# Interleaving the high and the low part of each weight chunk element by element in one tile, in a fp32 decoder trunk

## The chip, the cores and the metric

The kernel runs on one core of a Trainium2 chip. The metric is the device time of one execution in microseconds (us), as the median of three runs; lower is better. Engines are named as in the profile: PE is the matmul engine and PEld its weight loads, DVE the vector engine, ACT the scalar engine, POOL the general one, and SP the engine from whose queue the weight transfers are issued.

## The reference

Two layers of a decoder block work on one sequence of 256 tokens with a width of 1024. A layer is a half-weighted SwiGLU feed-forward part (FFN), a mixer, and a second FFN; each is preceded by an RMS norm, and shifted, scaled and gated by vectors that are computed from a condition `c`. What matters of it:

```python
for l in range(DEPTH):
    mod = jnp.split(c_act @ w_ada[l] + b_ada[l], N_MOD, axis=-1)
    h = modulate(rms_norm(x, ffn1_norm[l]), mod[0], mod[1])
    x = x + FFN_RESIDUAL * (1 + mod[2])[:, None, :] * swiglu(h, ffn1_w_gu[l], ffn1_w_down[l])
    h = modulate(rms_norm(x, mix_norm[l]), mod[3], mod[4])
    y = hybrid_mixer(h, cos, sin, w_in[l], q_a_norm[l], w_uq[l], kv_a_norm[l], w_ukv[l],
                     conv_w[l], attn_out_norm[l], conv_out_norm[l], w_o[l])
    x = x + (1 + mod[5])[:, None, :] * y
    h = modulate(rms_norm(x, ffn2_norm[l]), mod[6], mod[7])
    x = x + FFN_RESIDUAL * (1 + mod[8])[:, None, :] * swiglu(h, ffn2_w_gu[l], ffn2_w_down[l])
return rms_norm(x, final_norm)
```

The mixer projects `h` once, sends one part of the columns through latent attention with 8 heads and the other through a gated convolution of three taps, norms both and projects the pair. All data are fp32, and so is the answer. The hidden width of a FFN is 2816.

## The kernel before

Features lie on the 128 partitions and tokens along the free dimension, so a weight tile of 128x128 is the stationary operand of a matmul and the activations of 256 tokens are the moving one.

**Three matmuls for one product.** Both operands are split into a high part, rounded to the type F32R (a reduced fp32 that PE multiplies in one pass), and a low part, the rest: w = hi + lo and a = aH + aL. `mm3` (L282) issues hi\*aH, hi\*aL and lo\*aH into the same accumulator, and leaves lo\*aL out. All of them go through `mm` (L277), whose line of issue, L279, is therefore the line of nearly all matmuls in the profile.

**The weight stream.** The weights come as chunks of 128x2048 fp32, 16 tiles each (1 MB). `load` (L234) takes the next chunk of a fixed list: it allocates a tile `raw` for the transfer and two tiles `hi` and `lo` for its parts, each of three buffers, issues the transfer on SP (L244), issues the condition's rows that are due (`ada`, L188, a multiply and sum on DVE over 128x1024), and splits the chunk in two or four pieces. For each piece ACT copies `raw` to `hi` (L254, in `top`), and DVE subtracts: `lo` = `raw` - `hi` (L257, in `rest`). The chunks of the first FFN come first, then those of the mixer, then those of the second FFN.

**Who reads hi and lo.** The projections, the FFNs and the attention's queries and keys read them as stationary operands. One place reads them as the moving operand: `values` (L629), where PE takes `ckvH` and `ckvL` as stationary tiles and streams 512 columns of `hi` or `lo`, twelve matmuls in each layer. Four tiles of each of the first eight chunks are not split at all, but multiplied from `raw` in full fp32.

**What sets the order.** The kernel gives each piece of work a due time (`due`, L273), counted in nominal matmul time, and a scheduler orders the instructions of ACT, DVE and (in the FFNs) PE by due time and by when their operands would be ready. SP's order is written by hand everywhere, PE's in the mixer, where it follows `ORDER` (L42). At the end of a mixer stands the output projection `out` (L743). Its last step (a `B` of `ORDER`) brings the last two of the eight residual tiles, `residual` (L373, its sum at L376), and `put` (L366) makes the next FFN's input from them: `uH` on ACT (L334) and `uL` on DVE (L340). The first chunk of that FFN starts before all of that input is there, since its matmuls take the feature tiles k = 0 to 7 in turn (L481 to L483).

Of the kernel before, what the change touches and what calls it, by code (L numbers as in the profile page):

```python
# [12 lines left out]
F32R = mybir.dt.float32r  # L13
# [5 lines left out]
P = 128  # L19
# [12 lines left out]
CH = 16 * P  # L32
# [86 lines left out]
def trunk(ctx: ExitStack, tc, x_d, c_d, pos_d, small_d, cst_d, ada_d, gu1_d, dn1_d, win_d, up_d, wo_d, gu2_d, dn2_d, out_d):  # L119
# [9 lines left out]
    def nm(s):  # L129
        uid[0] += 1  # L130
        return f"{s}_{uid[0]}"
# [11 lines left out]

# [1 line left out]
    x = one.tile([P, KD, S], F32, name="x")  # L145
# [23 lines left out]

# [1 line left out]
    mods = [one.tile([P, NA], F32, name=f"mod{l}") for l in range(L)]  # L171
# [19 lines left out]
    def ada_target(i):  # L191
        """Rows of the modulation that are due by chunk i."""
        for (a, u), (b, v) in zip(PACE, PACE[1:]):
            if i <= b:
                return min(u + (v - u) * max(i - a, 0) // (b - a), len(ADA_ORDER))
        return len(ADA_ORDER)
# [6 lines left out]
    def last_of():  # L203
        """The last instruction so far of the vector and the scalar engine."""
        o = nc.cur_bb.bb.instructions
        return [next(i for i in reversed(o) if i.engine == e) for e in (mybir.EngineType.DVE, mybir.EngineType.Activation)]

# [1 line left out]
    stream = []  # L209
# [24 lines left out]
    def load(apart=False):  # L234
        """Loads the next chunk and splits it, at once or by the functions that come with it."""
        i = taken[0]
        taken[0] += 1
        src, n, cuts = stream[i][:3]
        z0 = stream[i][3] if len(stream[i]) > 3 else 0
        raw = wp.tile([P, CH], F32, tag="raw", name=nm("raw"), bufs=3)  # L240
        hi = wp.tile([P, CH], F32R, tag="hi", name=nm("hi"), bufs=3)
        lo = wp.tile([P, CH], F32R, tag="lo", name=nm("lo"), bufs=3)
        due(-LOAD_LEAD)
        nc.sync.dma_start(raw[:, :n], src)  # L244
        due(lead[1])
        with ExitStack() as es:
            for q in guard:
                es.enter_context(tc.issue_after(q))
            ada(ada_target(i + 1))
        c = (n - z0) // cuts  # L250
        zs = [slice(z0 + q * c, z0 + (q + 1) * c) for q in range(cuts)]

        def top(q):
            nc.scalar.activation(hi[:, zs[q]], raw[:, zs[q]], AF.Copy)  # L254

        def rest(q):
            nc.vector.tensor_tensor(lo[:, zs[q]], raw[:, zs[q]], f32(hi[:, zs[q]]), ALU.subtract)  # L257

        if apart:
            return (raw, hi, lo), top, rest  # L260
        with ExitStack() as es:
            for q in guard:
                es.enter_context(tc.issue_after(q))
            for q in range(cuts):
                due(c / 128 * 322 * q - lead[0])
                top(q)
                rest(q)
        return raw, hi, lo
# [4 lines left out]
    def due(t):  # L273
        """What follows is wanted t ns after the matmuls so far."""
        tc.cur_priority = int(clock[0] + t)
# [14 lines left out]

# [1 line left out]
    class Stat:  # L292
        """Sum of squares over the features, then 1/sqrt(mean + eps) on every partition."""

# [15 lines left out]
        def rstd(self, r, ps=None, then=None, t=0):  # L310
            """Leaves 1/sqrt(mean + eps) in r, and the table of the function that is next."""
            more = ps is not None
# [16 lines left out]
    def warm(src, func):  # L329
        """Loads the table of func ahead of its use, once src is there."""  # L330
        nc.scalar.activation(work([P, 1], "warm", 2), src, func)
# [10 lines left out]
    class Pre:  # L342
        """Input of a sub-layer: x*g*(1+scale) in two parts, the shift in two more columns."""

# [26 lines left out]

# [1 line left out]
    def residual(src, m, l, sub, f):  # L373
# [12 lines left out]
    def ffn(l, sub, pre, nxt, first=False):  # L386
        def evac(j, pg, pu, r):
            """Activation of pair j from PSUM, in two parts."""
            sg = work([P, S], "cc", 3)
# [16 lines left out]
        if first:  # L406
            r = work([P, S], "r", 1)
# [124 lines left out]
    def mixer(l, pre, nxt):  # L532
# [12 lines left out]
        def scaled(pt):  # L545
            """Brings two tiles of the projection from PSUM."""
            b = work([P, 2], "pb", 4)
# [20 lines left out]
        def proj(t, evac):  # L568
            """A quarter of two tiles of the projection."""
            n = seen[t] = seen.get(t, -1) + 1  # L570
# [11 lines left out]

        # q and kv latents
        def kv_evac(gb):
# [23 lines left out]

        # keys without position, values
        def keys():  # L610
# [31 lines left out]

        # attention, two heads at a time
        hd = [dict() for _ in range(4)]
# [68 lines left out]

        # gated short convolution
        def conv_evac(gb):
# [23 lines left out]

        # output projection  # L740
        acc = []
# [37 lines left out]

# [1 line left out]
    def rope():  # L781
# [63 lines left out]

# [1 line left out]
    fin = Stat(D)  # L847
# [12 lines left out]
def _tiles(w):  # L860
    """[.., K, M] -> [.., K/128, M/128, 128, 128]"""
    k, m = w.shape[-2:]
    w = w.reshape(w.shape[:-2] + (k // P, P, m // P, P))
    return np.swapaxes(w, -3, -2)
# [72 lines left out]
```

## Time and profile before

| what | us |
|---|---|
| median of 3 runs | 1005.36 (1004.75 to 1005.51) |
| span of the profiled execution, first to last instruction | 1002.8 |
| median less span: what lies around the span | 2.6 |
| PE busy | 976.1 |
| DVE busy | 809.7 |
| ACT busy | 551.5 |
| `lo` on DVE (L257), 384 instructions | 394.8 |
| `hi` on ACT (L254), 384 instructions | 338.4 |

A group's row names the line, the engine, the operation, the tile written and the tiles read, the shapes and the count, and after the bar the busy time in us, the mean of one in ns, and the idle time of the engine just before it. A row of a window names the stretch in us, and for each engine its busy time and its number of instructions in it. A row of the timeline begins with the start in us and the duration. Records of matmuls overlap, as PE is pipelined, so the pace is read from their starts or their number in a window, and not from their durations.

### The profile page before, as it was taken

How to read it: one execution, taken by the hardware profiler on the slowest of the kernel's cores; microseconds unless marked ns; L12 is line 12 of the kernel's file. 1: busy time of each engine (PE TensorE's matmuls, PEld its weight loads, DVE VectorE, ACT ScalarE, POOL GpSimd, SP SyncE). 2: the span in 40 equal slices, each digit the busy share in tenths (PEclk: the TensorE clock that was granted, in tenths of full speed). 3: DMA queues.
4: the chain of work that ended last, by engine and by line, in shares of the span. 5: the costliest groups of instructions: out<-in, count | busy, mean ns of one | idle time of the engine just before them, and what ended most of it. 6: DMA issues, size and time to landing. Idle time of an engine off the chain costs nothing.

```text
span 1002.8 us, 19512 instructions
## 1 busy us (share of the span) xinstructions
PE 976.1 (97%) x7982; PEld 960.6 (96%) x7982; DVE 809.7 (81%) x1518; ACT 551.5 (55%) x958; POOL 8.0 (1%) x27
## 2 busy tenths in 40 slices
PE   6999999999989999999999999999999999999996
PEld 4999999999989999999999999999998999999996
DVE  5999999899999987777889777778898998645452
ACT  5464544468856744454475444445787585444441
POOL 0000020000000000000000000000000000000000
PEclk9999999999999999999999999999999999999999
DMA  8989889873755678777758778776464447554531
GB/s 329 367 343 359 315 320 348 292 297 138 275 182 210 262 297 292 261 289 273 277 226 313 270 261 292 283 270 228 149 226 189 169 174 307 193 198 181 179 116 42
DMA packets 46442, 250.42 MB, mean 250 GB/s; under 512 B 5441, under 2 KB 5761, under 8 KB 25874
## 3 DMA queue, kind: packets, MB, share of 16 engines
q1 hardware_dynamic: 45938, 248.95, 67.4%
q8 instruction: 62, 1.02, 0.4%
q0 software_dynamic: 416, 0.25, 0.1%
q14 instruction: 26, 0.21, 0.1%
HBM read 248.07 MB, written 1.10 MB: 248 GB/s over the span
## 4 chain that ended last, share of the span: by engine, by line
PE 92%; DVE 5%; issue 1%; ACT 1%; DMA 1%; SPq 0%; DVEq 0%
PE ps L279 91%; DVE lo L257 1%; DMA x<-in_x 1%; PE ps L695 1%; DVE x L376 1%; DVE ada L188 0%; DVE acc L305 0%; DVE nt L558 0%; DVE mr L338 0%; DVE uL L340 0%; DVE rs_a L326 0%; ACT hi L254 0%; DVE rs_a L325 0%; ACT rs_y L321 0%; DVE y L383 0%
## 5 line engine op out<-in xcount | busy, mean ns | idle before, releaser
L279 PE MATMUL ps<-uH,hi 128*128 128x256 f32 (+1 forms) x1664 | 472.4, 284 | 0.0
L279 PE MATMUL ps<-uH,lo 128*128 128x256 f32 (+1 forms) x1664 | 469.4, 282 | 0.0
L279 PE MATMUL ps<-uL,hi 128*128 128x256 f32 x1664 | 465.5, 280 | 0.6 <-DVE uL L340 0.6
L257 DVE TENSOR_TENSOR lo<-raw,hi 128x1024 fp32r<-128x1024 f32 (+2 forms) x384 | 394.8, 1046 | 78.2 <-ACT hi L254 77.3
L254 ACT ACTIVATE hi<-raw 128x1024 fp32r<-128x1024 f32 (+2 forms) x384 | 338.4, 913 | 214.2 <-PE ps L279 134.0
L279 PEld LDWEIGHTS ps<-uL,hi 128*128 128x128 f32 x1664 | 315.1, 189 | 1.5 <-DVE uL L340 1.0
L279 PEld LDWEIGHTS ps<-uH,lo 128*128 128x128 f32 x1664 | 313.6, 188 | 0.0
L279 PEld LDWEIGHTS ps<-uH,hi 128*128 128x128 f32 x1664 | 312.5, 188 | 1.1 <-issue 0.3
L188 DVE CUSTOM_DVE_ANT_0 ada<-ada,cb,small 128x1024 f32<-128x1024 f32 x144 | 182.9, 1280 | 47.1 <-DMA ada<-in_ada 47.0
L279 PE MATMUL ps<-aH,hi 128*128 128x256 f32 x704 | 199.5, 283 | 0.0
L279 PE MATMUL ps<-aL,hi 128*128 128x256 f32 x704 | 197.8, 281 | 0.0
L279 PE MATMUL ps<-aH,lo 128*128 128x256 f32 x704 | 197.7, 281 | 0.0
L279 PEld LDWEIGHTS ps<-aL,hi 128*128 128x128 f32 x704 | 132.5, 188 | 0.0
L279 PEld LDWEIGHTS ps<-aH,hi 128*128 128x128 f32 x704 | 132.3, 188 | 0.0
L279 PEld LDWEIGHTS ps<-aH,lo 128*128 128x128 f32 x704 | 132.1, 188 | 0.0
L279 PE MATMUL ps<-mr,hi 128*128 128x256 f32 x384 | 73.2, 291 | 6.2 <-ACT mr L334 3.1
L279 PEld LDWEIGHTS ps<-mr,hi 128*128 128x128 f32 x384 | 61.4, 195 | 8.4 <-ACT mr L334 3.5
L334 ACT ACTIVATE aH<-cc 128x256 fp32r<-128x256 f32 x88 | 36.3, 415 | 55.6 <-DVE cc L392 51.9
L279 PE MATMUL ps<-mr,lo 128*128 128x256 f32 x192 | 55.0, 287 | 0.0
L334 ACT ACTIVATE uH<-x,gs 128x256 fp32r<-128x256 f32 x40 | 20.2, 505 | 57.7 <-DVE x L376 57.7
L376 DVE SCALAR_TENSOR_TENSOR x<-ps,gate,x 128x256 f32<-128x256 f32 x48 | 22.4, 480 | 25.6 <-PE ps L279 25.6
L391 ACT ACTIVATE cc<-ps 128x256 f32<-128x256 f32 x76 | 27.9, 368 | 24.4 <-PE ps L279 23.5
(117 smaller groups left out, 622.0 us busy)
## 6 DMA issues: line engine op xcount, KB each, us to landing
raw<-in_gu SPq DMA_DIRECT2D x88, 1024.0 KB, 5.3
ada<-in_ada SPq DMA_DIRECT2D x144, 512.0 KB, 6.0
raw<-in_dn SPq DMA_DIRECT2D x44, 1024.0 KB, 5.4
raw<-in_win SPq DMA_DIRECT2D x18, 1024.0 KB, 5.1
raw<-in_wo SPq DMA_DIRECT2D x8, 1024.0 KB, 4.9
raw<-in_up SPq DMA_DIRECT2D x2, 1024.0 KB, 5.2
raw<-in_up SPq DMA_DIRECT2D x2, 768.0 KB, 5.2
raw<-in_up SPq DMA_DIRECT2D x4, 384.0 KB, 3.3
```

The lines of the kernel that those rows point to most:

```text
L188: nc.vector.tensor_tensor_reduce(out=a, in0=a, in1=cb, scale=1.0, scalar=sm(l, t), op0=ALU.mult, op1=ALU.add, accum_out=mods[l][:, t:t + 1])
L254: nc.scalar.activation(hi[:, zs[q]], raw[:, zs[q]], AF.Copy)
L257: nc.vector.tensor_tensor(lo[:, zs[q]], raw[:, zs[q]], f32(hi[:, zs[q]]), ALU.subtract)
L279: nc.tensor.matmul(dst, a, b, **kw)
L334: nc.scalar.activation(dH, src, AF.Copy, scale=scale)
L376: nc.vector.scalar_tensor_tensor(x[:, m, :], src, g, x[:, m, :], ALU.mult, ALU.add)
L391: nc.scalar.activation(sg, pg, AF.Silu)
L695: nc.tensor.transpose(ps[:, e, z], d["e"][:, e, z], ident)
```

## The change

`load` allocates one tile `both` of 128x2048x2 F32R values in place of the two tiles. Element 0 of each pair is the high part and element 1 the low part, so `hi` and `lo` are views of the same tile with a step of two elements, 8 bytes.

```diff
         raw = wp.tile([P, CH], F32, tag="raw", name=nm("raw"), bufs=3)
-        hi = wp.tile([P, CH], F32R, tag="hi", name=nm("hi"), bufs=3)
-        lo = wp.tile([P, CH], F32R, tag="lo", name=nm("lo"), bufs=3)
+        both = wp.tile([P, CH, 2], F32R, tag="hl", name=nm("hl"), bufs=3)
+        hi, lo = both[:, :, 0], both[:, :, 1]
```

The rest of the code is the same, apart from comments; the bytes of SBUF are the same too. Every reader and writer of a part now steps over the other part: the copy to `hi` on ACT writes with that step, the subtraction on DVE reads one operand and writes its result with it, and the weight loads of PE read with it, as do the moving operands of `values`.

The number of instructions on each engine and what they do is unchanged, and the order on SP and POOL too. On ACT, DVE and PE the scheduler places some instructions differently. On DVE the first such place is in the first layer's first FFN, behind the last steps of the rope tables. `lo` and `hl` are the low part of a chunk (L257), `cc` and `aL` belong to the activation of a pair of hidden tiles (L392 and L338), `ada` is a row of the condition (L188) and `gs` a column of scales. Before:

```order
L783 SCALAR_TENSOR_TENSOR ro_806<-ro_812 128x32
L188 ISA ada_1451,mod_87<-ada_1451,cb,small 128x1024
L188 ISA mod_87 128x1
L392 TENSOR_TENSOR cc_1312<-ps_1263,cc_1312 128x256
L257 TENSOR_TENSOR lo_1449<-raw_1447,hi_1448 128x1024
L338 TENSOR_TENSOR aL_622<-cc_1312,aH_621 128x256
L257 TENSOR_TENSOR lo_1449<-raw_1447,hi_1448 128x1024
```

With the change, at the same place:

```order
L783 SCALAR_TENSOR_TENSOR ro_795<-ro_801 128x32
L392 TENSOR_TENSOR cc_1295<-ps_1246,cc_1295 128x256
L188 ISA ada_1431,mod_87<-ada_1431,cb,small 128x1024
L188 ISA mod_87 128x1
L338 TENSOR_TENSOR aL_614<-cc_1295,aH_613 128x256
L257 TENSOR_TENSOR hl_1429<-raw_1428,hl_1429 128x1024 x2
```

The activation of the pair now stands ahead of the condition's row and of both halves of the chunk's low part, where it stood between them. The same exchange is seen in the rows that follow, and on ACT.

On PE the order differs where the first layer's mixer hands over to its second FFN. The tile `mr` holds the inputs of the output projection, so `mr` rows are its last step (24 matmuls), and rows with `uH` and `uL` are the FFN's first chunk. Before, the seam where that step begins, with 15 matmuls of the FFN ahead of it:

```order
L279 MATMUL ps_3843<-uH,hi_3833 128x258 [waits Activation_49]
L279 MATMUL ps_3843<-uL,hi_3833 128x256 [waits DVE_49]
L279 MATMUL ps_3843<-uH,lo_3834 128x258
L279 MATMUL ps_3508<-mr_2422,hi_3612 128x256 [waits DVE_49]
L279 MATMUL ps_3508<-mr_2422,hi_3612 128x256
L279 MATMUL ps_3508<-mr_2422,lo_3613 128x256
```

With the change, 24 matmuls of the FFN stand ahead of it:

```order
L279 MATMUL ps_3792<-uL,hl_3783 128x256
L279 MATMUL ps_3792<-uH,hl_3783 128x258
L279 MATMUL ps_3460<-mr_2389,hl_3563 128x256 [waits DVE_49]
L279 MATMUL ps_3460<-mr_2389,hl_3563 128x256 x23
L279 MATMUL ps_3792<-uH,hl_3783 128x258 [waits Activation_49]
L279 MATMUL ps_3792<-uL,hl_3783 128x256 [waits DVE_49]
```

So nine matmuls of the FFN moved ahead of the mixer's last step. In the second layer one matmul moved in the same way.

## Prediction

> **What bounds the kernel now.** I read the page first, for the busy times and the chain that ended last, then the windows, for the stages.
>
> ```profile
> span 1002.8 us, 19512 instructions
> PE 976.1 (97%) x7982; PEld 960.6 (96%) x7982; DVE 809.7 (81%) x1518; ACT 551.5 (55%) x958; POOL 8.0 (1%) x27
> PE 92%; DVE 5%; issue 1%; ACT 1%; DMA 1%; SPq 0%; DVEq 0%
> 20.00:60.00 40.00, 40.00 (x299) 38.73 (x298) 35.77 (x63) 21.17 (x31) 0.00 (x0) 1.00 0.93 352
> 60.00:210.00 150.00, 150.00 (x1258) 149.82 (x1257) 139.27 (x271) 72.82 (x119) 6.69 (x13) 1.00 0.88 333
> 210.00:300.00 90.00, 86.96 (x694) 83.30 (x694) 84.22 (x210) 66.56 (x151) 0.40 (x4) 1.00 0.57 205
> 300.00:500.00 200.00, 198.59 (x1663) 197.92 (x1662) 168.65 (x284) 107.27 (x170) 0.00 (x0) 1.00 0.73 270
> 500.00:700.00 200.00, 200.00 (x1681) 199.89 (x1680) 159.83 (x262) 103.50 (x162) 0.00 (x0) 1.00 0.73 268
> 700.00:900.00 200.00, 196.68 (x1599) 192.57 (x1598) 164.88 (x348) 128.39 (x253) 0.20 (x2) 0.99 0.55 200
> 900.00:1003.00 103.00, 93.78 (x783) 92.98 (x781) 47.26 (x65) 40.91 (x60) 0.00 (x0) 0.98 0.38 133
> ```
>
> The columns of a window are its length, then busy time and count of PE, PEld, DVE, ACT and POOL, the granted clock, and the DMA's share and rate. PE is the bound: it carries 92% of the chain, and from 60 to 900 us it lacks only 3.0 + 1.4 + 3.3 = 7.7 us, in the windows with the two mixers. Its pace in the first of the long windows is 150 us / 1258 = 119.2 ns for a matmul, at full granted clock. Beside it DVE is the next: 139.27 of 150 us there, so 10.7 us to spare, but 31 to 40 us in each of the three windows of 200 us. ACT has half of its time free.
>
> **What the change does, part by part.** No instruction is added or taken away; four kinds of access now step over 8 bytes for each fp32 value, and some instructions stand in another order. So the sum is one of prices of a step. I take each kind in turn: the weight loads, the copies and subtractions, the moving operands, the order.
>
> ```profile
> L279 PEld LDWEIGHTS ps<-uL,hi 128*128 128x128 f32 x1664 | 315.1, 189 | 1.5 <-DVE uL L340 1.0
> L279 PEld LDWEIGHTS ps<-uH,lo 128*128 128x128 f32 x1664 | 313.6, 188 | 0.0
> L279 PEld LDWEIGHTS ps<-uH,hi 128*128 128x128 f32 x1664 | 312.5, 188 | 1.1 <-issue 0.3
> L279 PEld LDWEIGHTS ps<-aL,hi 128*128 128x128 f32 x704 | 132.5, 188 | 0.0
> L279 PEld LDWEIGHTS ps<-aH,hi 128*128 128x128 f32 x704 | 132.3, 188 | 0.0
> L279 PEld LDWEIGHTS ps<-aH,lo 128*128 128x128 f32 x704 | 132.1, 188 | 0.0
> L279 PEld LDWEIGHTS ps<-mr,hi 128*128 128x128 f32 x384 | 61.4, 195 | 8.4 <-ACT mr L334 3.5 <-DVE x L376 2.5 <-DVE mr L338 1.4
> L279 PEld LDWEIGHTS ps<-mr,lo 128*128 128x128 f32 x192 | 37.4, 195 | 0.0
> L279 PEld LDWEIGHTS ps<-mf,qh 128*128 128x128 f32 x64 | 9.2, 191 | 0.9 <-issue 0.3
> L279 PEld LDWEIGHTS ps<-pT,mf 128*64 128x64 f32 x64 | 4.0, 136 | 2.5 <-ACT cc L554 0.7
> 235.68 0.39 PE L279 MATMUL ps<-lo,mr 128*128 128x512 f32 x1
> 236.37 0.39 PE L279 MATMUL ps<-lo,mr 128*128 128x512 f32 x1
> ```
>
> *Weight loads.* The first eight rows are the loads of `hi` and `lo`: 3 x 1664 + 3 x 704 + 384 + 192 = 7680. One load stands to each matmul and runs beside the one before, so a load that comes to stick out by 1 ns costs 7.7 us in all. No row has a stepped load. Lower bound: 0. Upper bound: the stream of a load doubles. The last two load rows give that stream: 64 columns more take 191 - 136 = 55 ns, 0.86 ns a column, 110 ns for 128; so at most 7680 x 110 ns = +845 us. I take 0, by the moving operand as the nearest row. In `values` (the two timeline rows) three matmuls of 512 columns take 236.37 - 235.68 = 0.69 us, so PE draws a contiguous row of fp32 at 0.45 ns a value, or 8.9 bytes of address range per ns. A stepped load at its present pace covers 8 bytes in 0.86 ns, 9.3 per ns, nearly the same. If what costs is how much of a partition's memory a port crosses in a ns, a load is at a rate that another port of the same engine already keeps up.
>
> ```profile
> L257 DVE TENSOR_TENSOR lo<-raw,hi 128x1024 fp32r<-128x1024 f32 x252 | 304.8, 1219 | 74.0 <-ACT hi L254 73.4 <-issue 0.3
> L257 DVE TENSOR_TENSOR lo<-raw,hi 128x512 fp32r<-128x512 f32 x104 | 67.0, 684 | 1.1 <-ACT hi L254 0.9
> L783 DVE TENSOR_TENSOR ro<-ro,ro 128x32 f32<-128x32 f32 x2 | 0.4, 183 | 0.0
> L364 DVE TENSOR_TENSOR uH<-mod,uH 128x8 fp32r<-128x8 f32 x5 | 0.8, 167 | 0.0
> L254 ACT ACTIVATE hi<-raw 128x1024 fp32r<-128x1024 f32 x252 | 260.8, 1053 | 195.0 <-PE ps L279 126.0 <-issue 65.8 <-DMA raw<-in_dn 1.6
> L254 ACT ACTIVATE hi<-raw 128x512 fp32r<-128x512 f32 x104 | 58.0, 619 | 13.0 <-PE ps L279 5.4 <-issue 3.5 <-DMA raw<-in_win 2.8
> L363 ACT ACTIVATE uH<-mod 128x8 fp32r<-128x8 f32 x5 | 1.0, 204 | 1.3 <-DVE mod L188 1.3
> L331 ACT ACTIVATE warm<-cc 128x1 f32<-128x1 f32 x4 | 0.8, 203 | 0.0
> ```
>
> *Subtractions on DVE.* A column costs (1219 - 684) / 512 = 1.045 ns now, so the stepped access covers 8 / 1.045 = 7.7 bytes per ns, less than the moving operand. Lower bound: 0. The nearest stepped row is L364, which reads one operand and writes its result with a step of a whole row (258 values), on 8 values. By L783 a contiguous one of 8 would take 183 - 24 x 1.045 = 158 ns; it takes 167, so 9 / 8 = 1.1 ns a value more. That is the upper bound, with a far longer step and a count so small that the 9 ns may be something else. I take 0; what a price would do is the first rival. The Trainium skill, page "SBUF — State Buffer", section "Specifications (TRN2)", says that memory lines are 16 bytes and two hits in a line are enough for full bandwidth. By that, a step of 8 bytes, which hits each line twice, is free on every engine, the sum stays as it is, and L364, whose step leaves the line, would pay, as its 9 ns allow.
>
> *Copies on ACT.* (1053 - 619) / 512 = 0.85 ns a column, 9.4 bytes per ns when stepped. L363 writes 8 values with the long step in 204 ns, where L331 writes a single one in 203, so its row shows no price: lower bound 0; upper bound a doubling, 0.85 ns x 329,728 columns (252 x 1024 + 104 x 512 and 28 smaller pieces) = 280 us more work on an engine with 451 us free. I take 0.
>
> *Moving operands.* Of all matmuls 24 take 512 stepped values as moving operand, at 0.23 us each. Here the stepped access would cover 17.8 bytes per ns, twice what any row shows. Lower bound 0, upper bound a doubling: 24 x 0.23 = +5.5 us, straight on PE, which runs without a break there. I take 0 as the likeliest and hold the 5.5 us as a case of its own.
>
> *The order.* In the FFNs a chunk's split comes ahead of its use by more than an exchange of two instructions of 0.4 and 1.2 us; from 500 to 700 us PE never stops. At the mixers' end there is no such cover:
>
> ```profile
> 319.09 0.87 DVE L376 SCALAR_TENSOR_TENSOR x<-ps,gate,x 128x256 f32<-128x256 f32 x2
> 319.88 1.22 DVE L257 TENSOR_TENSOR lo<-raw,hi 128x1024 fp32r<-128x1024 f32 x1
> 321.54 0.39 PE L279 MATMUL ps<-uL,hi 128*128 128x256 f32 x1 [0.27 <-DVE uL L340]
> ```
>
> PE already waits 0.27 us for the last `uL`, which comes from the last residual by way of DVE, behind a subtraction. With nine matmuls put ahead of the step that brings the residual, 9 x 0.119 = 1.1 us, that `uL` comes up to 1.1 us later, and nothing else is left for PE to do meanwhile; in the second layer it is 0.1 us. Lower bound: -0.3 us (the wait goes), upper bound +1.2 us. DVE's order is new there too; I take the middle, +0.7 us.
>
> *Sum.* 1002.8 + 0 + 0 + 0 + 0 + 0.7 = 1003.5 us of span, and 2.6 us around it (the median of 1005.36 less the span) give 1006.1, so **1006 us**. About 0.2%, 2 us, is what a measurement of this kernel tells from no change.
>
> **The rivals.**
>
> *DVE becomes the bound (slower).* Place: the first FFN, 60 to 210 us, then every window up to 900. The first window holds some 51,700 columns of subtraction (61.5 us by the first row below, at 1219 / 1024 = 1.19 ns with the fixed part), so the point from which it decides is 10.7 us / 51,700 = 0.21 ns more a column, a fifth more.
>
> ```profile
> 60.00:210.00 150.00, 61.50 (x54) 1.00 0.88 333
> 300.00:500.00 200.00, 84.97 (x72) 1.00 0.73 270
> 500.00:700.00 200.00, 85.13 (x76) 1.00 0.73 268
> 700.00:900.00 200.00, 78.45 (x86) 0.99 0.55 200
> 900.00:1003.00 103.00, 33.68 (x28) 0.98 0.38 133
> L257 DVE TENSOR_TENSOR lo<-raw,hi 128x1024 fp32r<-128x1024 f32 (+2 forms) x384 | 394.8, 1046 | 78.2 <-ACT hi L254 77.3
> ```
>
> The first five rows are L257's share of DVE, the last its whole. At 1.1 ns more, each of these times grows by 1.1 / 1.19 = 92%. DVE then needs 196 us in the first window, and 247, 238 and 237 in the next three; after 900 us it has room. The rest, 394.8 - 343.7 = 51.1 us, lies nearly all between 20 and 60 and between 210 and 300 us; it grows by 47, where DVE has 130 - 120 = 10 us to spare. That is 46 + 47 + 38 + 37 + 37 = +205 us, 1211 in all. At half the price it is 18 + 8 + 0 + 1 + 13 = +40 us, 1046. For it: two of the three operands are stepped, and L364 may show a price. Against: the same row is tiny, and 7.7 bytes per ns is the slowest of the four kinds of access. The Trainium skill, page "Vector Engine (DVE) Microarchitecture Reference", section "5.2 Measured stream behaviour on trn2 (trn3 not measured)", speaks for this rival: a port keeps its full rate only over runs of two adjacent words, and a result that hops at every value took 1.71 ns a column against 1.05. An estimate by these figures, 0.66 ns more, would put this kernel near 1077 us. That page and the other disagree for a step of two words, and no row here settles it. Chance 0.17.
>
> *The weight loads stick out (slower).* If a stepped load takes 13 ns longer than the present pace hides, a ninth of 119 ns, it costs 100 us (1106); a doubled stream 845 us (1851). For it: PE has nothing to hide it behind, and 119.2 ns is only 4 ns above what 256 columns take at 0.45 ns (115), so a load that is nearly as long as its matmul has little slack. Against: the range per ns, above. Chance 0.14.
>
> *Only the moving operands pay (slower).* 1006.1 + 5.5 = 1011.6. For it: twice the highest rate that any row shows. Against: that the highest rate shown is the limit isn't shown. Chance 0.20.
>
> *The new order frees PE (faster).* At most the 7.7 us that PE lacks between 60 and 900 us could go: 998 to 1003. Against: these waits hang on activations and norms, which the change leaves as they are, and at the one seam that I can follow it goes the other way. Chance 0.06.
>
> That the change doesn't do what it says is not a case here: the order shows one tile in the place of two at every reader.
>
> **How the numbers follow.** No price that can be measured has 0.43 and is the likeliest single case; its own range is 1004 to 1008. The slower cases together hold more, 0.17 + 0.14 + 0.20 = 0.51; faster 0.06. So the likeliest case's own range is not the range: that goes from 1003, which cuts off most of the faster case, to 1106, which holds the moving operands, DVE at up to about half its price and somewhat more, and the loads at 13 ns. Left out are about 0.05 of DVE's chance, 0.08 of the loads', and 0.04 below.
>
> **What would show it.** Right: L257 and L254 of 128x1024 stay at 1219 and 1053 ns, the pace in a FFN window stays at 119 ns, the matmuls of 512 columns keep 0.23 us. Wrong in the first rival: L257 above 1430 ns and PE waits on `lo` from 60 us on. Wrong in the second: the pace of every window grows alike, with DVE's rows unchanged. Wrong in the third: only the starts of the 24 lie further apart. The order's term is read at the seam near 321 us. The forecast is wrong as a whole if the FFN windows, which hold most of the time, change their pace at all.

## The result, and the profile after

The changed kernel takes 1021.99 us (1021.23 to 1022.58, 4 runs) against 1005.15 us (1004.75 to 1005.51, 4 runs) for the kernel before: a ratio of 1.017, interval 1.0158 to 1.0182, slower by 16.8 us. The profiled execution grew by 1019.9 - 1002.8 = 17.1 us.

Below is the page of the changed kernel (span, busy times, shares of the chain), and then its windows, with the columns as in the prediction.

```profile
span 1019.9 us, 19504 instructions
PE 994.1 (97%) x7982; PEld 973.8 (95%) x7982; DVE 815.0 (80%) x1518; ACT 578.2 (57%) x958; POOL 8.0 (1%) x27
PE 95%; DVE 3%; ACT 1%; DMA 1%; issue 0%; SPq 0%; DVEq 0%
```

```profile
60.00:210.00 150.00, 150.00 (x1245) 149.80 (x1244) 138.43 (x267) 76.73 (x116) 6.72 (x13) 1.00 0.87 331
300.00:500.00 200.00, 197.71 (x1633) 196.97 (x1633) 166.32 (x284) 111.44 (x169) 0.00 (x0) 1.00 0.71 262
500.00:700.00 200.00, 200.00 (x1664) 199.95 (x1664) 162.04 (x261) 107.76 (x158) 0.00 (x0) 1.00 0.73 269
```

PE was the bound and is it more than before: 95% of the chain in place of 92%. Its busy time grew by 18.0 us, about what the span grew by. In the first and the last of these windows it still runs without a break, in the middle one it lacks 2.3 us where it lacked 1.4, and the granted clock is full in all three; but it starts fewer matmuls: 1245 in place of 1258, 1633 in place of 1663, 1664 in place of 1681. What PE is idle in the whole span went from 26.7 to 25.8 us. So the time went into the pace, not into waits. The rows of the changed kernel for the split and for the two largest groups of loads:

```profile
L257 DVE TENSOR_TENSOR hl<-raw,hl 128x1024 fp32r<-128x1024 f32 x252 | 304.5, 1222 | 48.8 <-ACT hl L254 47.7
L254 ACT ACTIVATE hl<-raw 128x1024 fp32r<-128x1024 f32 x252 | 286.4, 1163 | 77.7 <-issue 59.2 <-PE ps L279 13.8 <-ACT sq L301 2.0
L279 PEld LDWEIGHTS ps<-uH,hl 128*128 128x128 f32 x3328 | 531.9, 197 | 2.8 <-ACT uH L334 1.9 <-issue 0.3
L279 PEld LDWEIGHTS ps<-uL,hl 128*128 128x128 f32 x1664 | 327.9, 197 | 1.2 <-DVE uL L340 0.7
```

DVE pays nothing (1222 against 1219 ns). ACT pays 110 ns for a copy, a tenth (1163 against 1053), and its busy time grows by 27 us; it has over 400 us free, and carries 1% of the chain as before. A load's record is 8 ns longer (197 against 189).

Where the pace changed is read from shorter windows that hold one kind of work each: 520 to 620 us only gate and up projections (moving operands `uH` and `uL`), 155 to 200 us only a down projection (`aH` and `aL`). The rows count the matmuls of L279; first the kernel before, then the changed one:

```profile
155.00:200.00 45.00, 45.00 (x380) 45.00 (x379) 1.00 0.84 309
520.00:620.00 100.00, 100.00 (x845) 100.00 (x844) 1.00 0.75 281
```

```profile
155.00:200.00 45.00, 45.00 (x381) 45.00 (x380) 1.00 0.82 314
520.00:620.00 100.00, 100.00 (x828) 99.95 (x827) 1.00 0.74 270
```

Gate and up slow down (845 to 828 in 100 us), the down projection doesn't. From the single starts in the trace the mean distance is finer than a count: worked out over the same windows, it goes from 118.65 to 121.2 ns in gate and up, and from 119.26 to 118.88 ns in down.

The third place is `values`. The twelve matmuls of 512 stepped columns in the first layer, with the row of PE behind them:

```profile
237.49 5.76 PE L279 MATMUL ps<-hl,mr 128*128 128x512 f32 x12
243.07 1.14 PE L279 MATMUL ps<-mr,hl 128*128 128x256 f32 x8
```

They hold PE for 243.07 - 237.49 = 5.58 us, 0.465 us each, where the prediction read 0.23.

### The profile page after: what moved, and what is told of

Its sections match the earlier page's. It is cut to its first block, busy times and chain, and to the rows that moved or that the text cites. A ratio compares the mean times of both kernels' runs of the same rounds, so it can differ in the third digit from the quotient of the medians.

```text
span 1019.9 us, 19504 instructions
## 1 busy us (share of the span) xinstructions
PE 994.1 (97%) x7982; PEld 973.8 (95%) x7982; DVE 815.0 (80%) x1518; ACT 578.2 (57%) x958; POOL 8.0 (1%) x27
## 4 chain that ended last, share of the span: by engine, by line
PE 95%; DVE 3%; ACT 1%; DMA 1%; issue 0%; SPq 0%; DVEq 0%
PE ps L279 94%; DMA x<-in_x 1%; DVE hl L257 1%; PE ps L695 1%; DVE nt L558 0%; DVE mr L338 0%; ACT hl L254 0%; DVE ada L188 0%; DVE x L376 0%; DVE rs_a L326 0%; DVE rs_a L325 0%; ACT rs_y L321 0%; DVE y L383 0%; DVE rh L327 0%; DVE g L550 0%
## 5 line engine op out<-in xcount | busy, mean ns | idle before, releaser
L279 PE MATMUL ps<-uH,hl 128*128 128x256 f32 (+1 forms) x3328 | 615.5, 286 | 1.5 <-ACT uH L334 1.5
L279 PEld LDWEIGHTS ps<-uH,hl 128*128 128x128 f32 x3328 | 531.9, 197 | 2.8 <-ACT uH L334 1.9
L279 PE MATMUL ps<-uL,hl 128*128 128x256 f32 x1664 | 472.6, 284 | 0.3
L257 DVE TENSOR_TENSOR hl<-raw,hl 128x1024 fp32r<-128x1024 f32 (+2 forms) x384 | 394.9, 1049 | 55.8 <-ACT hl L254 54.5
L254 ACT ACTIVATE hl<-raw 128x1024 fp32r<-128x1024 f32 (+2 forms) x384 | 370.4, 1005 | 99.4 <-issue 64.7
L279 PEld LDWEIGHTS ps<-uL,hl 128*128 128x128 f32 x1664 | 327.9, 197 | 1.2 <-DVE uL L340 0.7
L279 PE MATMUL ps<-aH,hl 128*128 128x256 f32 x1408 | 251.8, 283 | 0.0
L279 PEld LDWEIGHTS ps<-aH,hl 128*128 128x128 f32 x1408 | 221.1, 196 | 0.0
L188 DVE CUSTOM_DVE_ANT_0 ada<-ada,cb,small 128x1024 f32<-128x1024 f32 x144 | 183.1, 1280 | 40.8 <-DMA ada<-in_ada 40.7
L279 PE MATMUL ps<-aL,hl 128*128 128x256 f32 x704 | 196.1, 279 | 0.0
L279 PEld LDWEIGHTS ps<-aL,hl 128*128 128x128 f32 x704 | 138.6, 197 | 0.0
L279 PE MATMUL ps<-mr,hl 128*128 128x256 f32 x576 | 76.8, 293 | 6.0 <-ACT mr L334 3.2
L279 PEld LDWEIGHTS ps<-mr,hl 128*128 128x128 f32 x576 | 73.8, 202 | 8.9 <-ACT mr L334 3.6
L392 DVE TENSOR_TENSOR cc<-ps,cc 128x256 f32<-128x256 f32 x76 | 31.7, 422 | 41.2 <-ACT cc L391 40.9
L338 DVE TENSOR_TENSOR aL<-cc,aH 128x256 fp32r<-128x256 f32 x88 | 36.7, 419 | 1.2 <-ACT aH L334 0.6
L279 PE MATMUL ps<-cc,raw 128*128 128x256 f32 x64 | 17.0, 413 | 3.0 <-DVE cc L445 3.0
```

Source lines behind the costliest of these rows:

```text
L188: nc.vector.tensor_tensor_reduce(out=a, in0=a, in1=cb, scale=1.0, scalar=sm(l, t), op0=ALU.mult, op1=ALU.add, accum_out=mods[l][:, t:t + 1])
L279: nc.tensor.matmul(dst, a, b, **kw)
L338: nc.vector.tensor_tensor(dL, src, f32(dH), ALU.subtract)
L392: nc.vector.tensor_tensor(sg, pu, sg, ALU.mult)
```

## The experiments

Ratios and intervals are against the kernel before on the same chip. A span is that of one execution, the profiled one; the executions of one kernel lie 0.6 to 5.8 us apart, so a difference of spans is to be read beside that of the medians. The distances of starts in the table are worked out from the starts in each trace, in ns, over the two windows named above.

| kernel | median, us | ratio (interval) | span, us | gate/up | down |
|---|---|---|---|---|---|
| before | 1005.15 | | 1002.8 | 118.65 | 119.26 |
| changed | 1021.99 | 1.017 (1.0158 to 1.0182) | 1019.9 | 121.21 | 118.88 |
| e_halves | 1007.13 | 1.0016 (1.0007 to 1.0026) | 1003.8 | 118.67 | 119.25 |
| e_only_values | 1013.44 | 1.0079 (1.0062 to 1.0096) | 1012.9 | 118.67 | 119.26 |
| e_all_but_values | 1016.34 | 1.0111 (1.0096 to 1.0126) | 1014.7 | 121.00 | 118.89 |
| e_only_gu | 1016.66 | 1.0108 (1.0087 to 1.013) | 1013.7 | 121.00 | 119.26 |
| e_starts | 993.26 | 0.9875 (0.9855 to 0.9896) | 992.0 | 118.60 | 113.33 |
| e_starts_step | 1024.63 | 1.0192 (1.0166 to 1.0218) | 1021.4 | 121.21 | 120.00 |
| e_starts_u | 1000.29 | 0.9945 (0.9924 to 0.9965) | 1001.0 | 119.06 | 113.33 |

**One tile without the step (e_halves).** The tile, its buffers and the order of the changed kernel, with the two parts side by side:

```diff
-        both = wp.tile([P, CH, 2], F32R, tag="hl", name=nm("hl"), bufs=3)
-        hi, lo = both[:, :, 0], both[:, :, 1]
+        both = wp.tile([P, 2, CH], F32R, tag="hl", name=nm("hl"), bufs=3)
+        hi, lo = both[:, 0, :], both[:, 1, :]
```

> One tile holds both parts as in the changed kernel, but as two halves, so no access steps. Theory A (the step costs: 24 stepped moving operands at +0.22 us = 5.3 us, and 4992 matmuls on uH and uL at +2.4 ns = 12 us): both go, 1005 us, pace 118.6 ns in a gate-and-up window, copy on ACT back at 1053 ns. Theory B (one tile and the new order cost, by waits and by other neighbours in time): it stays near 1022 us. Both in part: between.

Measured: 1007.13 us, a ratio of 1.0016, and both paces of the kernel before. Its windows:

```profile
155.00:200.00 45.00, 45.00 (x379) 45.00 (x379) 1.00 0.83 310
520.00:620.00 100.00, 100.00 (x845) 100.00 (x845) 1.00 0.75 280
```

So one tile and the new order cost 1.0 us of span and 2.1 us by the medians, with 0.7 to 2.6 us as the interval of the ratio. The rest, 16.1 us of span and 14.9 us by the medians, comes from the step.

**The step where it is a moving operand, and everywhere else (e_only_values, e_all_but_values).** A list of the stream's chunks by kind says which of them interleave; the others have halves. In the first kernel only the two chunks of `values` ("v") do, in the second all the others ("gdm"):

```diff
+        both = wp.tile([P, 2 * CH], F32R, tag="hl", name=nm("hl"), bufs=3)
+        if kind[i] in "v":
+            pair = both.rearrange("p (c t) -> p c t", t=2)
+            hi, lo = pair[:, :, 0], pair[:, :, 1]
+        else:
+            hi, lo = both[:, :CH], both[:, CH:]
```

> Only the two chunks that the attention's values are taken from are interleaved; all others lie in two halves. Theory A: the 24 moving operands pay alone, 1005.2 + 5.3 = 1010.5 us, each at 453 ns. Theory B: whatever one tile for all costs, 1022 us, or 1005 if the order is as before.

> All chunks are interleaved but for the two of the attention's values. Theory A: 1022.0 - 5.3 = 1016.7 us, the values' matmuls back at 231 ns, the pace of gate and up still 121.0 ns. Theory B: 1022 us. If the prices do not add, the two kernels with one part each do not sum to 16.8 us.

Measured: 1013.44 and 1016.34 us. With the step in all chunks but those of `values`, PE's rows at the place shown above are (L279 is L295 there, behind the list of kinds):

```profile
237.58 3.12 PE L295 MATMUL ps<-hl,mr 128*128 128x512 f32 x12
240.54 3.64 PE L295 MATMUL ps<-mr,hl 128*128 128x256 f32 x29
```

The twelve take 240.54 - 237.58 = 2.96 us in place of 5.58, which is 2.6 us in a layer and 5.2 in both; the changed kernel's span is 5.2 us longer than this one's. The other way round, e_only_values adds 9.1 us to the span of e_halves. By the distances of starts 5.3 of them arise at the two places of `values`; 1.1 arise ahead of the 250th matmul and the other 2.7 in later stretches, with no change of either pace. In the later stretches PE waits for `uL` on DVE where an FFN hands over to the next part, 0.7 us at 517 and 0.9 us at 705, and in e_halves it doesn't. By the medians the two kernels are only 6.3 us apart, so most of the 3.8 us may be no more than the difference of one execution from another. The forecast of 1010.5 had no term for the one tile, which by the medians costs 2.1 us.

**The step alone, outside the kernel (e_probe).** Each kind of access by itself: 96 matmuls of 256 columns, or 48 of 512, back to back, with a stepped load or a stepped moving operand; six copies on ACT and six subtractions on DVE of 1024 columns for each step. An excerpt:

```python
nc.tensor.matmul(pf[:, 512:768], step(W, 2, 128), M[:, 0:256], start=True, stop=True)  # load step 2
nc.tensor.matmul(pf[:, 512:1024], W[:, 0:128], step(M, 2, 512), start=True, stop=True)  # moving step 2
nc.tensor.matmul(pf[:, 512:1024].rearrange("p (a b) -> p a b", b=2), W[:, 0:128], pairs(M, 512), start=True, stop=True)
```

> Leaves out the model: it times the accesses by themselves, on random data, first six copies on ACT and six subtractions on DVE for each step, then 96 (or 48) equal matmuls for each kind of access, one source line each. Theory A1 (a port that crosses more than about 9 bytes of a partition's row per ns slows down): weight load with step 2 keeps the pace of step 1, step 4 and 8 are slower by a multiple; a moving operand with step 2 doubles (256 columns 107 to 213 ns, 512 columns 213 to 430), step 4 quadruples or stays at the double; pairs of neighbours (two values, then a gap of two) cross as much as step 2 and double too. Theory A2 (a port fetches 8 bytes at a time and what counts is the number of fetches): pairs cost nothing, step 2 and step 4 both double. On ACT, step 2 costs 0.1 ns a value more in writing (1163 against 1053 ns of the changed kernel); on DVE nothing (1222 against 1219), and step 4 more on both. If the pace of 121.0 ns comes from the stepped load meeting the moving operand at certain addresses, the lines with an offset or with rows of 258 differ by some ns at step 2.

In the rows for one line, the two times behind the durations are the first and the last start in us, so the pace is their difference over the count less one. L77, L79 and L83 are loads at step 1, 2 and 4 with 256 columns; the others have 512 columns: L87 with all contiguous, L89 with the load at step 2, L99, L101 and L103 with the moving operand at step 2, at step 4, and as pairs of adjacent values.

```profile
L77 PE MATMUL ps<-M,W x96: 283/283/283, 90.0 to 101.4; 128*128 128x256 f32 x96
L79 PE MATMUL ps<-M,W x96: 278/283/285, 101.5 to 112.9; 128*128 128x256 f32 x96
L83 PE MATMUL ps<-M,W x96: 393/396/402, 129.7 to 151.8; 128*128 128x256 f32 x96
L87 PE MATMUL ps<-M,W x48: 389/389/392, 175.2 to 185.9; 128*128 128x512 f32 x48
L89 PE MATMUL ps<-M,W x48: 394/394/398, 186.1 to 197.1; 128*128 128x512 f32 x48
L99 PE MATMUL ps<-M,W x48: 629/631/652, 273.7 to 295.0; 128*128 128x512 f32 x48
L101 PE MATMUL ps<-M,W x48: 639/642/643, 295.5 to 317.2; 128*128 128x512 f32 x48
L103 PE MATMUL ps<-M,W x48: 629/631/652, 317.6 to 339.0; 128*128 128x512 f32 x48
```

Groups of DVE (contiguous; both stepped by 2; result stepped by 4) and of ACT (step 1, 2 and 4 in the result) in the same kernel:

```profile
L57 DVE TENSOR_TENSOR D<-raw,W 128x1024 fp32r<-128x1024 f32 x6 | 7.3, 1224 | 0.2
L63 DVE TENSOR_TENSOR D<-raw,D 128x1024 fp32r<-128x1024 f32 x6 | 7.4, 1226 | 0.2
L65 DVE TENSOR_TENSOR D<-raw,W 128x1024 fp32r<-128x1024 f32 x6 | 12.0, 1993 | 0.2
L45 ACT ACTIVATE D<-raw 128x1024 fp32r<-128x1024 f32 x6 | 6.3, 1054 | 0.2
L47 ACT ACTIVATE D<-raw 128x1024 fp32r<-128x1024 f32 x6 | 6.8, 1141 | 0.2
L49 ACT ACTIVATE D<-raw 128x1024 fp32r<-128x1024 f32 x6 | 12.4, 2070 | 0.2
```

The load's pace is 11.4 / 95 = 120 ns at step 1 and at step 2, and 22.1 / 95 = 233 ns at step 4. So at this place, with the moving operand begun at the start of its tile as the weights are, a load at step 2 has no price with 256 columns, which leaves the 2.4 ns of the kernel open. With 512 columns it has one even here: from the single starts 226.7 ns at step 1 and 233.3 at step 2. The moving operand goes from 10.7 / 47 = 228 to 21.3 / 47 = 453 ns at step 2. It takes the same as pairs, and 461 ns at step 4: what doubles it is not how much memory it crosses but that it isn't contiguous. DVE is free at step 2 and pays at step 4; ACT pays 8% at step 2 and doubles at step 4.

**Where the moving operand begins (e_probe2, e_probe3).** In gate and up the starts in the kernel's trace repeat their pattern of distances from chunk to chunk, every 48 matmuls, to within a ns, so I took the pace for a matter of addresses. The second probe begins a contiguous moving operand of 256 columns at 0, 4, 8, ... 128 values behind the weights, with loads at step 1 and at step 2; the third takes the kernel's triples (hi with H, hi with L, lo with H) with H and L begun at all pairs of such places, at step 1:

```python
nc.tensor.matmul(pf[:, 512:768], step(W, 1, 128), M[:, 28:28+256], start=True, stop=True)  # load step 1, moving offset 28
nc.tensor.matmul(pf[:, 512:768], step(W, 2, 128), M[:, 28:28+256], start=True, stop=True)  # load step 2, moving offset 28
```

> Leaves out the model: PE alone, equal matmuls of 256 columns in groups of 48 or 96, one source line each. The start of the moving operand is shifted against the start of the weights by 0 to 128 values in steps of 4, with weight loads of step 1 and of step 2; then groups of three as the model has them (high part with two moving operands, low part with the first), for several starts and row lengths. Theory A3 (PE's two reads meet in the same part of the memory, and what decides is the distance of the two addresses): at step 1 the pace goes up and down with the shift between 113 and 127 ns and repeats after 128 values, as the six shifts of the probe before showed (113.3 ns at 32, 126.7 at 4); at step 2 it stays between 118 and 121 whatever the shift; the threes show about the mean of their pairs, with rows of 258 near 118.6 at step 1 and 121.0 at step 2, as the two kernels have. Rival (the load alone sets the pace, and the shifts of the probe before were an accident of its order): all shifts of one step give the same pace, 120 ns, and the threes too.

> Leaves out the model: PE alone, groups of three matmuls as the model has them, all with weight loads of step 1, for 16 x 16 starts of the two moving operands (aH and aL, or uH and uL) against the weights, 0 to 60 values in steps of 4, and for rows of 258 and 264 of the first one. Theory A3 (the distance of the addresses decides, per pair of a load and a running matmul): the pace of a three is near the mean of the paces that its shifts had alone, 113 to 120 ns, so the 256 means spread over some ns; with 48 and 0, as the second weight matrix of the FFN has them, 119.3 ns; with rows of 258 at 0 and 16, as the first has them, 118.6 ns; and some pairs of starts give 115 ns or less, from which a faster layout could be made. Rival (the shifts alone were an accident of what ran before them): the means of the same starts scatter about 119 ns without order, and neither 119.3 nor 118.6 comes back at those places.

The places that the first of these texts quotes from the first probe, 32 and 4 values, are in its code 16 (113.3 ns) and 2 (126.7 ns). Each probe ran once, with PE alone, at a granted clock of 0.999 or 1.0.

Rows of the second probe: step 1 at 0, at 28 and at 32 values (L52, L66, L68), step 2 at 0 and 28 (L118, L132), step 1 with the weights begun 96 values on and the moving operand at 0 (L194), and triples with rows of 258 as `uH` has them, at step 1 and at step 2 (L200, L218). Then a row of the third probe, the triples at 28 and 28 values.

```profile
L52 PE MATMUL ps<-M,W x48: 283/283/283, 23.4 to 29.1; 128*128 128x256 f32 x48
L66 PE MATMUL ps<-M,W x48: 275/275/275, 63.4 to 68.7; 128*128 128x256 f32 x48
L68 PE MATMUL ps<-M,W x48: 274/281/287, 68.8 to 74.4; 128*128 128x256 f32 x48
L118 PE MATMUL ps<-M,W x48: 278/283/285, 210.3 to 216.0; 128*128 128x256 f32 x48
L132 PE MATMUL ps<-M,W x48: 278/280/288, 250.5 to 256.1; 128*128 128x256 f32 x48
L194 PE MATMUL ps<-M,W x48: 274/281/287, 428.6 to 434.2; 128*128 128x256 f32 x48
L200 PE MATMUL ps<-M,W x96: 277/281/288, 451.5 to 462.8; 128*128 128x256 f32 x96
L218 PE MATMUL ps<-M,W x96: 277/283/292, 554.2 to 565.6; 128*128 128x256 f32 x96
```

```profile
L290 PE MATMUL ps<-M,W x48: 275/275/282, 698.3 to 703.7; 128*128 128x256 f32 x48
```

From the single starts, at step 1 the pace is 120.0 ns at 0 values, 113.3 at 28 and at 48, and between 116.7 and 120.0 at the other places; it repeats exactly after 64 values, 256 B. At step 2 it is 120.0 at 0 and at 28, and over all places between 117.8 and 121.2. The place that the first probe used, 0, is thus one of the slowest of step 1; on the mean of the sixteen places a load at step 2 is 1.9 ns dearer, 119.8 against 117.9. The triples with rows of 258 go from 118.9 to 120.6 ns, with nothing on the other engines, where gate and up of the kernel go from 118.65 to 121.0. L194 takes 118.6 ns, which is the pace at 32 values (L68, 118.5), not that at 0: it is the distance between the two operands that counts, as far as this one pair tells.

The distance is not all, though. The first probe had a few of these places too, in another sequence. At 16 values it gave the first row below, the second probe the second:

```profile
L123 PE MATMUL ps<-M,W x96: 275/276/276, 443.2 to 453.9; 128*128 128x256 f32 x96
```

```profile
L60 PE MATMUL ps<-M,W x48: 279/279/284, 46.2 to 51.7; 128*128 128x256 f32 x48
```

From the single starts that is a steady 113, 113, 114 ns in the one and a steady pattern around 117.8 in the other, with the same addresses and step. So a run of matmuls settles into a repeating pattern, and which one depends on the addresses and on how it was entered. Over both probes the paces at step 1 go from 113.3 to 126.7 ns (at 2 values, in the first). Once settled, the triples lie between 113.3 (28 and 28; 114.0 over all 48) and 121.0 ns. The theory's rule for them, the mean of what their places take alone, fails: over the 256 pairs the two hardly go together (correlation 0.08). Triples whose two operands begin at the same place take 113.3 to 120.2 ns by where that place is, so it is not the distance of the two from each other that decides. Nor do the triples give the kernel's pace in general: its down projection has its operands at 48 and 0 values (by the sizes of the tiles ahead of them; a trace holds no addresses) and takes 119.26 ns, the probe's triple at 48 and 0 takes 117.8. In the kernel that projection repeats its pattern every 27 matmuls, which is not a chunk.

**The step in gate and up alone (e_only_gu).** As the edit above, with "g" in place of "v".

> Only the chunks of the gate and up projections keep the two parts alternating; the chunks of the down projection, of the block in the middle and of `values` have them as halves of the tile. Theory (a stepped load takes away the faster places of the moving operand's address, which shows with uH and uL): 1376 triples of matmuls on uH and uL lie in these chunks, 4128 matmuls at 121.0 in place of 118.6 ns, +9.9 us over the kernel with halves (1007.1), so 1016 to 1018. Rival (the slower pace comes from ScalarE's dearer copies or from the order, not from the load's step): spread over all chunks, 1009 to 1012.

Measured: 1016.66 us, and a span 1013.7 - 1003.8 = 9.9 us longer than that of e_halves, as worked out from the pace; by the medians it is 9.5 us. Its windows:

```profile
155.00:200.00 45.00, 45.00 (x380) 45.00 (x379) 1.00 0.85 320
520.00:620.00 100.00, 100.00 (x828) 100.00 (x828) 1.00 0.74 275
```

Gate and up have the changed kernel's 828, the down projection the 380 of before. The cost belongs to the chunks that are stepped. From kernel to kernel the spans go from 1002.8 us by 1.0 for one tile and its order, 9.9 for gate and up, 1.0 for the down projections and the middle block together (e_all_but_values) and 5.2 for `values` to 1019.9; that they add up is no test, since each step starts where the last one ends. The medians give 2.1, 9.5, -0.3 and 5.7 us. So the two large steps are clear of the scatter, and that of the down projections and the middle block is not.

**Other starts for the down projection's operands (e_starts, e_starts_step).** If the faster patterns are real, the kernel before can be brought into one, and the changed kernel should gain nothing by the same move. Both parts of the activation begin 112 B (28 values) behind the weights, mod 256 B, again by the sizes of the tiles:

```diff
-        aH = one.tile([P, NJ, S], F32R, tag="aH", name=nm("aH"))
-        aL = one.tile([P, NJ, S], F32R, tag="aL", name=nm("aL"))
+        aH = one.tile([P, NJ * S + 64], F32R, tag="aH", name=nm("aH"))[:, 44:44 + NJ * S].rearrange("p (j s) -> p j s", j=NJ)
+        aL = one.tile([P, NJ * S + 64], F32R, tag="aL", name=nm("aL"))[:, 28:28 + NJ * S].rearrange("p (j s) -> p j s", j=NJ)
```

> The kernel before, with aH and aL begun 112 B (mod 256 B) after the weights' start in place of 192 B and 0 B, nothing else moved. Theory (at step 1 the pace is set by the distance of moving operand and weights mod 256 B, and the pair 28/28 values of the third probe holds in the kernel): the 2112 matmuls of the down projections go at 113.5 in place of 119.26 ns, -12 us, 993. If the probe's pair doesn't carry over to the kernel, whose chunks, PSUM banks and columns differ: anywhere between 114 and 120 ns, 994 to 1007. Rival (addresses play no part, the pace was noise of the probe): 1005, pace 119.3.

> The changed kernel, with the same starts of aH and aL. Theory (at step 2 the faster places are gone): the down projections keep a pace of 118 to 121 ns, 1020 to 1026. If the faster pace at these starts is there at step 2 too: 113.5 ns, 1010.

Measured: 993.26 us for the first, faster than both kernels (ratio 0.9875, 0.9855 to 0.9896), and 1024.63 us for the second. The windows of the first, then of the second:

```profile
155.00:200.00 45.00, 45.00 (x400) 45.00 (x399) 1.00 0.86 333
520.00:620.00 100.00, 100.00 (x845) 100.00 (x844) 1.00 0.78 284
```

```profile
155.00:200.00 45.00, 45.00 (x378) 45.00 (x377) 1.00 0.83 309
520.00:620.00 100.00, 100.00 (x828) 99.95 (x827) 1.00 0.74 270
```

At step 1 the down projection starts 400 matmuls where it started 380, 113.33 ns from start to start, while gate and up keep their 845. At step 2, with the same starts, it is 120.00 ns. The same address is thus worth 5.9 ns a matmul at step 1 and costs 1.1 ns at step 2.

**All four operands moved (e_starts_u).** On the kernel before, with `uH` and `uL` begun at the same distance as well.

> The kernel before, with all four moving operands begun 112 B (mod 256 B) after the weights' start: aH and aL as in the run before, and uH (whose rows of 258 values shift by 8 B from row to row) and uL too. Theory (each pair of starts has a pace of its own): the down projections keep 113.5 ns; the 4128 matmuls of gate and up go at a pace that no probe gives, since uH's rows begin at eight places. The triples with rows of 258 lay between 117.9 and 119.7 ns in the third probe where the kernel has 118.6: 990 to 998 us. If a row's own place counts alone, the row of uH that begins at 28 values and uL gain (113.3 ns) and the others don't: about 985. Rival (only the distance between the two moving operands counts, not that to the weights): as the run before, 993.

Measured: 1000.29 us, 7 us slower than e_starts. The down projection keeps its 113.33 ns; gate and up gain nothing (119.06 ns in the same window). And PE waits more for `uH` at the seams; the first row of its waits in this kernel (in all, times, longest), the row in e_starts, and a window of this kernel behind the first of these waits:

```profile
PE ps L279 <- ACT uH L334: 5.7, 4, 2.0
```

```profile
PE ps L279 <- ACT uH L334: 0.3, 1, 0.3
```

```profile
313.00:317.00 4.00, 4.00 (x24) 4.00 (x23) 3.47 (x10) 1.09 (x4) 0.00 (x0) 0.58 0.69 209
```

That is 5.4 of the 9.0 us by which the spans differ. The order on PE is another one: in e_starts 15 matmuls of the FFN stand ahead of the mixer's last step at both seams, as in the kernel before, and in e_starts_u none does, so PE has nothing else to do there. Behind the first of these waits, of 2.0 us, the granted clock was 0.58 on the mean of 4 us, with 24 matmuls in place of the 33 that fit at 119 ns. So this run is no clean test of the starts, beyond the two paces. Why the scheduler set another order was not followed further.

## Why the prediction was right and wrong

The time lies in the range given, but not by the case held likeliest. That case, no price that can be measured, put 1006 us; it is off by 16 us. No case of the prediction gives 1022 us: the nearest, the moving operands alone, gives 1011.6, and the rest of the range was there for DVE and for a load that sticks out everywhere, neither of which came. That the range holds the time is luck.

- **Weight loads, taken at 0: the step that failed.** The prediction took the pace of 119.2 ns as one property of all matmuls, held beside it that a load at step 2 crosses no more memory in a ns than the moving operand does, and concluded that a stepped load is as good as a plain one. Where the first probe tried it, the load is as good with 256 columns, 120 and 120 ns, but that place is one of the slowest of step 1, and with 512 columns it is not as good, 233.3 against 226.7. The 119 ns were a mean over places. At step 1 the probes' matmuls settled at 113 to 127 ns, most below 120, by where the moving operand begins and by what ran before; at step 2 the probes found nothing below 117.8. Gate and up were somewhat faster than 120 ns at step 1, and lose that: 4 FFNs x 22 chunks x 16 tiles, less 8 x 4 tiles that aren't split, are 1376 triples, 4128 matmuls, by 2.4 ns (121.0 less 118.6) = 9.9 us, and e_only_gu measured 9.9 of span, 9.5 by the medians. The down projections, at 119.26 ns, had little to lose: 2112 matmuls by -0.4 ns = -0.8 us. Of the bounds, 0 to 845 us, the truth was near the lower end, but the mechanism had no place in the sum: the second rival had the pace growing everywhere alike, and it grew in one kind of work and fell a little in the other.
- **Moving operands, taken at 0, with the upper bound as a rival.** The upper bound came: +5.2 us against 5.5. The reason given for it, twice the highest range per ns that any row shows, does not hold: step 4 crosses twice as much again and takes 461 ns where step 2 takes 453. The rule "range per ns" should not have set a price; a doubling at any step is what the runs show.
- **Subtractions on DVE, taken at 0: right.** 1222 against 1219 ns, and 1226 against 1224 in the probe. The first rival didn't come. Of the two rules of the Trainium skill that were at odds here, the one of the page "SBUF — State Buffer", section "Specifications (TRN2)", gives this row: two hits in a line of 16 bytes are enough, and at step 4, with one hit, the price is there (1993). The hop at every value of the Trainium skill's page "Vector Engine (DVE) Microarchitecture Reference", section "5.2 Measured stream behaviour on trn2 (trn3 not measured)", 1.71 ns a column, is not seen at step 2; that figure is for a hop of 4 KiB. But the first rule is not free on every engine, as the prediction read it: the moving operand doubles at two hits in a line.
- **Copies on ACT, taken at 0: wrong in size, without weight.** 110 ns more for a copy of 1024, 27 us in all, and nearly all of it hidden: at the seam shown below PE's wait behind two copies is 1.20 us, where e_halves has 1.07.
- **The order, +0.7 us: right in size, with another engine.** e_halves costs 1.0 us of span (2.1 us by the medians), and by the starts 1.1 us of it arise at the first layer's seam. There PE waits 1.07 us in e_halves and 1.20 us, the upper bound, in the changed kernel; not for `uL` by way of DVE, as the prediction had it, but for `uH` on ACT, which stands behind two copies of a chunk. The first row is of e_halves, the others of the changed kernel:

```profile
321.88 0.38 PE L279 MATMUL ps<-uH,hl 128*128 128x258 f32 x1 [1.07 <-ACT uH L334]
325.03 2.19 ACT L254 ACTIVATE hl<-raw 128x1024 fp32r<-128x1024 f32 x2 [2.07 <-PE ps L279]
327.09 0.50 ACT L334 ACTIVATE uH<-x,gs 128x256 fp32r<-128x256 f32 x1
327.64 0.39 PE L279 MATMUL ps<-uH,hl 128*128 128x258 f32 x1 [1.20 <-ACT uH L334]
```

- **The point that was to show the forecast wrong** was named rightly: the FFN windows changed their pace. That it could be 2% rather than a ninth was not weighed, since the second rival asked what happens if the load is slower, not what the present pace consists of.

Shown is that the cost hangs on the step in the chunks that pay it, that PE alone pays most of it too (1.7 ns in the triples with rows of 258), that at step 1 the pace hangs on the operands' starts, and that the gain found at one pair of starts is absent there at step 2. That the loads and the streams of moving operands get in each other's way in memory, in a pattern that locks in, would fit all of this, but it is argued and not shown. Which rule gives the pace of a mixed sequence of operands stays open, and in the kernel few starts were tried.

## What to carry to other kernels

Before taking a pace for the engine's own, look at it stage by stage: two stages with the same instructions that differ by half a ns, or a pattern that repeats to the ns from chunk to chunk, are a hint that addresses are in it. And a probe at one place, here one of the slowest, can hide a price that the kernel pays. A step of two fp32 values has a price of its own for each reader: keep moving operands contiguous, and cost loads, moving operands, DVE and ACT apart. When PE is the bound, the start of a moving operand is a knob to try: here 112 B in place of 192 and 0 B took 1.2% off the kernel before.

## What the hardware showed that was not expected

- With plain loads, a matmul of 256 columns takes 113.3 to 126.7 ns by the distance of moving operand and weights, mod 256 B, and by how the sequence was entered; with loads at step 2, 117.8 to 121.2.
- A moving operand of fp32 that isn't contiguous takes twice the time at step 2, at step 4 and in pairs (453, 461 and 453 ns against 227 for 512 columns).
- Beside a matmul of 256 columns that begins at the same place, mod 256 B, a load at step 2 is free (120 ns), one at step 3 brings the pace to 173 ns and one at step 4 to 233 ns. On the mean of sixteen places a load at step 2 costs 1.9 ns, and beside 512 columns 6.7 ns.
